# Normalising x on VectorE, squares of x by tokens, four-column gate scales and a new order in a hybrid attention and gMLP block

## The chip, the cores and the metric

The kernel runs on one core of one Trainium2 chip. The metric is the device time of one execution in microseconds (us). The engines are PE (TensorE), DVE (VectorE), ACT (ScalarE), POOL (GpSimd) and SP (SyncE, which here only issues DMA). PEld is the loading of weights into PE.

## The reference

One layer over 1024 tokens of width 1024, all in float32. The normalised stream is projected once and feeds attention (8 query heads and 2 key/value heads of 64), a gated MLP that mixes positions inside chunks of 128 tokens, and the merge gates:

```python
h = rmsnorm(x, norm_gain)
q, k, v, gate_a, u_in, v_in, gate_b, g_merge = split(h @ w_in)
q = axial_rope(rmsnorm(q, q_gain)); k = axial_rope(rmsnorm(k, k_gain))
attn = softmax(q k^T / 8) v * silu(gate_a)
y_a = attn @ w_proj_attn
vv = layernorm(gelu(v_in), ln_v_gain, ln_v_bias)          # 8 chunks x 8 groups
v_mix = einsum('gij,bcjgd->bcigd', w_spatial, vv) + b_spatial
gm = gelu(u_in) * v_mix * silu(gate_b)
y_b = gm @ w_proj_gmlp
g = sigmoid(g_merge + b_merge)
x = x + (g[0] * y_a + g[1] * y_b) @ w_out
return rmsnorm(x, final_gain)
```

## The kernel before

**Precision.** Each float32 operand of a large product is split into a rounded high part and a remainder (`split`, `split16`, L302 and L303: high on ACT, remainder on DVE), and each product is three matmuls (`mm3`, L188 to L190: high x high, high x low, low x high).

**Stages, in order of time.** Positions are those of the profiled execution.

1. 0 to 43 us: `load_x(dt)` brings x transposed (features on partitions, `xT`), eight tiles of 128 features. Each is multiplied by the norm gain and split (L164, L165). The k/v projection (`kv`) runs tile by tile in two of the three large PSUM tiles (tag `S`). `nat_weight` loads and splits the gMLP weights. `add_square` squares each transposed tile (L178 on ACT, L176 on POOL for tiles 1 and 4) and sums the squares on DVE (L182). One matmul per 128 tokens (L265) then adds over the features, and `power_rstd` gives `rstd`, the inverse root per token (DVE L139, POOL L140).
2. 43 to 86 us: `rB` is half of `rstd` spread over all partitions. `v_group(0..3)` project the gMLP input (PE, tile `v`), and their GELU on ACT (L481, scaled by `rstd`) frees the PSUM tile. `load_pair(k)` brings two tiles of `xT` again (`xp`), `norm_part(dt)` multiplies one by `rB` (DVE L315 for tiles 0, 1 and 3, two halves on POOL, L318, for the others), and `norm_split(dt)` turns it into two float16 parts (`x16`, L302 and L303). Beside them run the tables and the normalisation of k (`head_norm`, `rope`), and `v_post` (layernorm of a chunk) and `spatial` (its position mixing). `scales` loads weight blocks and sums their squares on ACT to scale them before the float16 split.
3. 86 to 160 us: `prep_q(dt)` splits the weights of q; `q_group(0..3)` need all eight `x16` tiles and all of those weights. `k_transposes`, `q_norm`, `q_split` prepare the attention operands. `bias_term` adds a row sum of the mixing matrix (L497) to the position bias (L501).
4. 160 to 405 us: 64 calls of `scores` (logits, softmax on DVE and ACT, DMA transpose) and 32 of `mix`, with the gate projections `run_fill` and the weight preparation `prep_next` between them.
5. 405 to 650 us: `proj_b`, `x_chunk`, then eight `gate(i)`. `pair_weights(i)` loads the gate weights and gets their scale from `unit_scale`: four sums of squares, one matmul each (L292), a copy (L294), and POOL steps (L295 to L298). `proj_a` and `merge` follow.
6. 650 to 747 us: `out_weight`, `split_y`, the output projection, residual and final norm.

**What sets the order.** The program text is a long hand-written list of calls at the end. The build's planner takes that order as a priority, simulates the engines' times, and fixes for every engine its own order of instructions; an engine then runs strictly in that order. `tc.high_priority()` moves a block ahead. Tiles with one tag share a small number of buffers, and a tile that needs a buffer waits until the last reader of an older one is done: `xa` (4 buffers: squares, raw weights of `scales`, x16 of tiles 0 to 3), `wraw` (4: raw weights), `qT` (4: `xp`, `vst`, later the transposed q), `ptr` (2: `nl`, then the split weights of q), `X` (8: the split x, then x16 of tiles 4 to 7), PSUM `S` (3), `o` and `z` (1 each). Nearly all loads are issued by SP in one queue; those of the first `scales` by ACT.

Of the kernel before, what the change touches and what calls it, by code (L numbers as in the profile page):

```python
# [16 lines left out]
P = 128  # L17
# [13 lines left out]
def hybrid_block_kernel(  # L31
# [79 lines left out]
    ones = t2("ones")[:, 0:P]  # L111
    dve.memset(ones, 1.0)

# [38 lines left out]
    def load_x(dt):  # L152
        raw = t4("T16", f"xraw{dt}")
        t = tX(f"xhl{dt}")
        hi, lo = t[:, 0, :], t[:, 1, :]
        cuts = [slice(0, 256), slice(256, 512), H(1)] if dt == 0 else [H(0), H(1)] if dt < 3 else [slice(0, 1024)]
        for i, r in enumerate(cuts):
            nc.sync.dma_start(out=raw[:, r], in_=xT[C(dt), r])
            if dt == 0 and i == 0:
                nc.scalar.dma_start(out=cs, in_=cst[:, 0:C_BSP])  # L160
            if dt == 0 and i != 1:
                first_w(i // 2)
        for r in cuts:
            act.activation(hi[:, r], raw[:, r], AF.Copy, scale=gain[:, dt:dt + 1])  # L164
            dve.scalar_tensor_tensor(out=lo[:, r], in0=raw[:, r], scalar=gain[:, dt:dt + 1], in1=hi[:, r].bitcast(F32),  # L165
                                     op0=ALU.mult, op1=ALU.subtract)
        xh.append(hi)
        xl.append(lo)
        xraw0.append(raw)

    ssq = []

    def add_square(dt):
        t = t4("xa", f"xsq{dt}")
        if dt in SQPOOL:
            pool.tensor_tensor(out=t, in0=xraw0[dt], in1=xraw0[dt], op=ALU.mult)  # L176
        else:
            act.activation(t, xraw0[dt], AF.Square)  # L178
        if dt == 0:
            ssq.append(t)  # L180
        else:
            (pool if dt in ADPOOL else dve).tensor_tensor(out=ssq[0], in0=ssq[0], in1=t, op=ALU.add)  # L182
# [23 lines left out]
    for i in range(4):  # L206
        for j in range(2):
# [16 lines left out]
            if dt > 0:  # L224
                add_square(dt - 1)
                nat_weight(W_VIN, dt - 1)
            if dt == 7:
                add_square(7)
                nat_weight(W_VIN, 7)
# [27 lines left out]
    dve.tensor_scalar(out=gsc[:, 0:1], in0=ssp[:, 16:17], scalar1=2.0 ** -16, scalar2=1e-30, op0=ALU.mult, op1=ALU.add)  # L257
# [4 lines left out]
    sst = ps_o("sst")  # L262
    for tt in range(NT):
        with tc.high_priority():
            pe.matmul(sst[:, tt:tt + 1], ssq[0][:, C(tt)], ones[:, 0:1], start=(tt == 0), stop=(tt == NT - 1))  # L265
    power_rstd(rstd, sst[:, 0:NT], NT, 1.0 / D)
# [20 lines left out]
    def unit_scale(ss, n, name, tag="sc", bufs=3):  # L287

        nscale.append(name)
        pt = ps_oz(len(nscale), f"us{name}")  # L290
        for i in range(n):
            pe.matmul(pt[:, 0:1], mscale.broadcast_to([P, P]), ss[:, i:i + 1], start=(i == 0), stop=(i == n - 1))  # L292
# [12 lines left out]
    x16, xpair = {}, {}  # L305
# [14 lines left out]
    NPD = (0, 1, 3)  # L320

    def norm_split(dt):
# [3 lines left out]
        else:  # L326
            if dt % 2 == 0:
                x16["t"] = tX16(f"x16{dt}")
            t = x16["t"][:, dt % 2]
# [165 lines left out]
    def bias_term(h):  # L495
        pt = ps_o(f"wsum{h}")
        pe.matmul(pt, ones, wsr[h], start=True, stop=True)  # L497
        for t in (2 * h, 2 * h + 1):
            for g2 in range(2):
                rows = slice(64 * g2, 64 * g2 + 64)  # L500
                dve.scalar_tensor_tensor(  # L501
                    out=bsp[rows, C(t)], in0=pt[rows, C(2 * (t % 2) + g2)], scalar=cs[rows, C_LNB + t:C_LNB + t + 1],
                    in1=bsp[rows, C(t)], op0=ALU.mult, op1=ALU.add)
# [460 lines left out]
    v_group(0)  # L964
# [18 lines left out]
    Ak, Bk = (heads(t) for t in tabk)  # L983
    load_wsp(0)
    early = scales(["q"] + order[:4], ["xa"] * 8)
    load_pair(1)
    load_wsp(1)
    load_pair(2)
    load_pair(0)
    norm_part(3)  # L990
    v_group(1)
    ktmp = t4("vS", "ktmp")
    head_norm(kn, ktmp, 0, 8, "kf")
    v_group(2)
# [5 lines left out]
    rope(kn, ktmp, Ak, Bk, 8, 2)  # L1000
    norm_part(0)
    norm_split(0)
    norm_part(1)
# [37 lines left out]
    dve.tensor_tensor(out=v3, in0=v3, in1=vinv[:, None, :].broadcast_to([P, 8, 128]), op=ALU.mult)
# [19 lines left out]
    norm_split(7)  # L1061
# [3 lines left out]
    split(khl[0], khl[1], kn, act)  # L1065
    q_group(0)
    v_post(3)
    spatial(2)
    qT = [t8("qT", 4, f"qT{j}") for j in range(4)]
    k_transposes(0)  # L1070
# [4 lines left out]
    k_transposes(2)
    spatial(3)
    scales(order[4:6])
    k_transposes(3)
    q_group(1)
    spatial(5)  # L1080
    prep_next()
    spatial(4)
    q_group(2)
    q_split(0)
    prep_next()
    q_split(1)
    v_post(6)
    spatial(6)
    scales(order[6:8])
    v_post(7)  # L1090
    q_norm(1)
    prep_next()
    q_split(2)
    spatial(7)
    q_group(3)
    prep_next()
    q_split(3)
    v_affine(1)
    v_affine(0)
    scores(*hs[0])  # L1100
    prep_next()
    v_affine(3)
    prep_next()
    scales(order[10:12])
    scores(*hs[1])
    scores(*hs[2])
    scales(order[8:10])
    scores(*hs[3])
    v_affine(2)
    run_fill(*halves[0])  # L1110
    prep_next()
    scores(*hs[4])
    q_norm(2)
    run_fill(*halves[1])
    q_split(5)
    scores(*hs[5])
    scores(*hs[6])
    mix(*hs[0][:2])
    q_split(4)
# [4 lines left out]
    q_norm(3)  # L1124
    scores(*hs[10])
    scores(*hs[11])
    q_split(6)
    q_split(7)
    mix(*hs[4][:2])
    scores(*hs[12])  # L1130
    scores(*hs[13])
    mix(*hs[6][:2])
    run_fill(*halves[2])
    mix(*hs[8][:2])
    scores(*hs[14])
# [142 lines left out]
    gate(6)  # L1278
    pws[7] = pair_weights(7)
# [3 lines left out]
    split_y(0)  # L1283
# [112 lines left out]
```

## Time and profile before

| | |
|---|---|
| median of 3 runs | 746.68 us (745.58 to 747.12) |
| profiled execution | 748.41 us, of which 746.6 us span |
| instructions | 12013 |
| busy: PE, DVE, ACT, POOL | 713.0, 591.8, 452.6, 132.3 us |
| mean granted TensorE clock | 0.983 |
| moved by DMA | 93.98 MB, 55.46 MB of it read from HBM |

Busy time is the time in which at least one instruction of the engine runs; waiting is not in it. The granted clock is the share of full speed that PE was given. The span is counted from the first to the last instruction. A row of the busy time by stage gives start, end, length, and then busy microseconds and the number of instructions for each engine. A row of the waits names who was idle, and for whose instruction.

### The profile page before, as it was taken

What the parts mean: (1) busy time and instruction counts of PE and PEld (TensorE: products, weight loads), DVE (VectorE), ACT (ScalarE), POOL (GpSimd) and SP (SyncE); (2) the same over time, 40 slices, a digit from 0 to 9 for tenths busy, and PEclk for the clock granted to TensorE, in tenths of its full rate; (3) what the DMA queues carried; (4) which work ended last, traced back from release to release, by engine and by line L of the source; (5) the groups of instructions that cost most, each with busy time, mean ns of one, the idle gap of its engine ahead of it and who ended that gap; (6) DMA issues with size and microseconds to landing.
All of it is one profiled execution on the core that took longest, in us unless ns stands there. A gap on an engine that the chain in (4) does not pass through costs nothing.

```text
span 746.6 us, 12013 instructions
## 1 busy us (share of the span) xinstructions
PE 713.0 (95%) x4685; PEld 471.2 (63%) x4685; DVE 591.8 (79%) x824; ACT 452.6 (61%) x808; POOL 132.3 (18%) x118
## 2 busy tenths in 40 slices
PE   7989879889999999999999999999999999999996
PEld 7978636455556555666656787556464466478885
DVE  7859989879989999777977699889687898972323
ACT  8563468887688898677785477655463445531011
POOL 3027731332301020001110025202002010000000
PEclk9999979999999999999999999999999999999999
DMA  8690144437487996998889921130031013330202
GB/s 309 224 356 7 57 140 155 129 113 141 88 176 144 205 196 114 160 164 141 156 150 219 270 85 45 41 127 16 1 141 57 1 56 128 135 137 26 110 32 84
DMA packets 156360, 93.98 MB, mean 126 GB/s; under 512 B 135824, under 2 KB 136464, under 8 KB 156304
## 3 DMA queue, kind: packets, MB, share of 16 engines
q1 hardware_dynamic: 154864, 88.75, 47.4%
q10 hardware_dynamic: 1440, 4.47, 1.7%
q8 instruction: 36, 0.59, 0.3%
q14 instruction: 20, 0.16, 0.1%
HBM read 55.46 MB, written 4.19 MB: 80 GB/s over the span
## 4 chain that ended last, share of the span: by engine, by line
PE 47%; DVE 20%; DMA 11%; ACT 10%; issue 7%; POOL 4%; SPq 1%; POOLq 0%; DVEq 0%; ACTq 0%
DMA T<-p 5%; PE out L189 4%; PE out L190 4%; PE out L188 4%; DVE p L651 4%; DVE nm L640 3%; PE g L188 3%; PE g L190 3%; PE g L189 3%; ACT p L650 2%; DMA sqq<-in_wall_dram 2%; DMA xraw<-in_xT_dram 2%; ACT P L644 2%; PE o L663 1%; DMA wraw<-in_wall_dram 1%
## 5 line engine op out<-in xcount | busy, mean ns | idle before, releaser
L651 DVE SCALAR_TENSOR_TENSOR p<-P,ri,p 128x1024 f16<-128x1024 f32 x64 | 83.4, 1307 | 18.2 <-ACT p L650 17.9
L644 ACT ACTIVATE P<-s,nm 128x1024 f32<-128x1024 f32 x64 | 71.2, 1113 | 27.6 <-DVE nm L640 23.6
L650 ACT ACTIVATE p<-P,ri 128x1024 f16<-128x1024 f32 x64 | 72.8, 1143 | 17.3 <-DVE ri L647 11.6
L640 DVE TENSOR_REDUCE nm<-s 128x1 f32<-128x1024 f32 x64 | 77.4, 1212 | 1.3 <-PE s L638 1.3
L637 PE MATMUL s<-kT,qT 128*128 128x512 f32 x128 | 56.7, 443 | 3.5 <-ACT P L644 2.7
L663 PEld LDWEIGHTS <-vS 128*64 128x64 f16 x1536 | 45.4, 110 | 18.0 <-issue 17.7
L663 PE MATMUL o<-T,vS 128*64 128x128 f16 x1536 | 52.8, 220 | 1.3 <-DMA T<-p 0.9
L638 PE MATMUL s<-kT,qT 128*128 128x512 f32 x128 | 50.8, 397 | 0.0
L923 ACT ACTIVATE sq<-xr 128x1024 f32<-128x1024 f32 x7 | 7.4, 1063 | 63.5 <-DVE xr L1326 63.2
L1326 DVE TENSOR_TENSOR xr<-out,xr 128x1024 f32<-128x1024 f32 x7 | 8.6, 1225 | 45.9 <-PE out L190 45.7
L295 POOL TENSOR_SCALAR scg<-scg 128x1 f32<-128x1 f32 x8 | 7.0, 871 | 190.7 <-ACT scg L294 110.4
L189 PE MATMUL out<-wo,yhl 128*128 128x512 f32 x96 | 37.4, 392 | 0.0
L188 PE MATMUL out<-wo,yhl 128*128 128x512 f32 x96 | 37.3, 392 | 0.0
L190 PE MATMUL out<-wo,yhl 128*128 128x512 f32 x96 | 37.3, 390 | 0.0
L188 PE MATMUL g<-x,wg 128*128 128x512 f16 x96 | 36.4, 379 | 0.0
L189 PE MATMUL g<-x,wg 128*128 128x512 f16 x96 | 36.4, 379 | 0.0
L190 PE MATMUL g<-x,wg 128*128 128x512 f16 x96 | 36.4, 379 | 0.0
L188 PE MATMUL q<-wq,x 128*128 128x512 f16 x64 | 25.5, 398 | 10.1 <-ACT vst L481 7.5
L637 PEld LDWEIGHTS s<-kT,qT 128*128 128x128 f32 x128 | 24.3, 190 | 12.1 <-ACT P L644 3.8
L188 PE MATMUL v<-nh,xhl 128*128 128x512 f32 x64 | 25.8, 403 | 2.5 <-DVE vn L238 2.5
L596 POOL TENSOR_TENSOR vm<-vm,ut 128x512 f32<-128x512 f32 x8 | 13.4, 1675 | 82.7 <-DVE ut L382 42.3
L302 ACT ACTIVATE wg<-graw,scg 128x512 f16<-128x512 f32 x16 | 11.6, 722 | 26.3 <-PE g L190 12.9
(548 smaller groups left out, 2113.4 us busy)
## 6 DMA issues: line engine op xcount, KB each, us to landing
wraw<-in_wall_dram SPq DMA_DIRECT2D x75, 256.0 KB, 3.3
graw<-in_wall_dram SPq DMA_DIRECT2D x16, 512.0 KB, 5.0
xraw<-in_xT_dram SPq DMA_DIRECT2D x13, 512.0 KB, 5.2
xp<-in_xT_dram SPq DMA_DIRECT2D x8, 512.0 KB, 8.7
wor<-in_wall_dram SPq DMA_DIRECT2D x8, 512.0 KB, 4.5
xr<-in_x_dram SPq DMA_DIRECT2D x8, 512.0 KB, 4.4
out_dram<-xr SPq DMA_DIRECT2D x7, 512.0 KB, 2.6
sqq<-in_wall_dram ACTq DMA_DIRECT2D x4, 512.0 KB, 5.8
```

What stands on the lines that cost most here:

```text
L188: pe.matmul(o, ah, bh, start=start, stop=False)
L189: pe.matmul(o, ah, bl, start=False, stop=False)
L190: pe.matmul(o, al, bh, start=False, stop=stop)
L302: act.activation(hi, raw, AF.Copy, scale=sc)
L596: pool.tensor_tensor(out=vm[:, et, H(h)], in0=vm[:, et, H(h)], in1=t, op=ALU.mult)
L637: pe.matmul(sp[:, H(hf)], qs, kT[v][:, 0, H(hf)], start=True, stop=False)
L638: pe.matmul(sp[:, H(hf)], qs, kT[v][:, 1, H(hf)], start=False, stop=True)
L640: dve.tensor_reduce(out=nm, in_=sp, axis=AX.X, op=ALU.max, negate=True)
L644: act.activation(Pt, sp, AF.Exp, bias=nm, accum_out=rsum)
L650: act.activation(hi, Pt, AF.Copy, scale=ri)
L651: dve.scalar_tensor_tensor(out=lo, in0=Pt, scalar=ri, in1=hi, op0=ALU.mult, op1=ALU.subtract)
L663: pe.matmul(ot[64 * h:64 * h + 64, 0:128], vS[:, kt, v, 64 * vl:64 * vl + 64], T[:, h, 8 * p + kt, :], start=(n == 0), stop=(n == len(part ...
```

## The change

The tokens' sums of squares are taken from x itself (tokens on partitions), loaded a second time in eight tiles; ACT squares and sums each, and neither DVE adds nor matmuls are left in it. All eight `norm_part` run on DVE. `unit_scale` does one matmul of four columns, and ACT sums the four columns while it copies. `bias_term` gets both 64-row halves of a tile in place with two masked matmuls of 256 columns, so that one DVE operation serves 128 rows. `gsc` has another constant (a scale). `x16` tiles 4 to 7 may be made in any order. The list of calls is reordered from `v_group(0)` to the output weights.

```diff
-    ones = t2("ones")[:, 0:P]
+    onz = t2("ones")[:, 0:P + 64]
+    ones = t2("one")[:, 0:P]
     dve.memset(ones, 1.0)
+    dve.memset(onz, 1.0)
+    dve.memset(onz[:, 64:P], 0.0)
...
-    def add_square(dt):
-        t = t4("xa", f"xsq{dt}")
-        if dt in SQPOOL:
-            pool.tensor_tensor(out=t, in0=xraw0[dt], in1=xraw0[dt], op=ALU.mult)
-        else:
-            act.activation(t, xraw0[dt], AF.Square)
...
-            (pool if dt in ADPOOL else dve).tensor_tensor(out=ssq[0], in0=ssq[0], in1=t, op=ALU.add)
+    ssx = const([P, NT], "ssx")
+    def add_square(tt):
+        xn = t4("xa", f"xn{tt}")
+        nc.sync.dma_start(out=xn, in_=x[C(tt), :])
+        act.activation(xn, xn, AF.Square, accum_out=ssx[:, tt:tt + 1])
...
             if dt > 0:
-                add_square(dt - 1)
                 nat_weight(W_VIN, dt - 1)
+            if dt > 3:
+                add_square(2 * dt - 8)
+                add_square(2 * dt - 7)
...
-    sst = ps_o("sst")
-    for tt in range(NT):
-        with tc.high_priority():
-            pe.matmul(sst[:, tt:tt + 1], ssq[0][:, C(tt)], ones[:, 0:1], start=(tt == 0), stop=(tt == NT - 1))
-    power_rstd(rstd, sst[:, 0:NT], NT, 1.0 / D)
+    power_rstd(rstd, ssx, NT, 1.0 / D)
...
-        for i in range(n):
-            pe.matmul(pt[:, 0:1], mscale.broadcast_to([P, P]), ss[:, i:i + 1], start=(i == 0), stop=(i == n - 1))
+        pe.matmul(pt[:, 0:n], mscale.broadcast_to([P, P]), ss, start=True, stop=True)
         sc = sb.tile([P, 2], F32, tag=tag, bufs=bufs, name=f"sc{name}")
-        act.copy(sc[:, 1:2], pt[:, 0:1])
+        act.activation(pt[:, 8:8 + n], pt[:, 0:n], AF.Copy, accum_out=sc[:, 1:2])
...
-    NPD = (0, 1, 3)
+    NPD = range(8)
...
-        pe.matmul(pt, ones, wsr[h], start=True, stop=True)
+        w4 = wsr[h].rearrange("p (t g i) -> p t g i", t=2, g=2)
+        for g2 in range(2):
+            pe.matmul(pt[:, 0:256], onz[:, 64 * g2:64 * g2 + P], w4[:, :, g2, :], start=(g2 == 0), stop=(g2 == 1))
         for t in (2 * h, 2 * h + 1):
-            for g2 in range(2):
-                rows = slice(64 * g2, 64 * g2 + 64)
-                dve.scalar_tensor_tensor(... 64 rows, 128 columns ...)
+            dve.scalar_tensor_tensor(... 128 rows, 128 columns ...)
```

The list of calls up to `q_group(0)`, before and after (calls that are not named stand where they stood):

```
before: v_group(0), tables, load_wsp(0), scales(q and 4 more), load_pair(1), load_wsp(1), load_pair(2), load_pair(0),
  norm_part(3), v_group(1), head_norm(k), v_group(2), scales_end, rope(k), norm_part(0), norm_split(0), norm_part(1),
  norm_split(1), v_group(3), norm_part(5), bias_term(0), v_post(0), spatial(0), v_post(1), spatial(1), bias_term(1),
  norm_split(3), prep_q(0..3), norm_part(2), prep_q(4), norm_part(4), prep_q(5), prep_q(6), norm_split(2), prep_q(7),
  norm_split(4), load_pair(3), norm_part(6), norm_split(5), norm_part(7), v_post(2), norm_split(6), norm_split(7), q_group(0)
after: tables, scales(q and 4 more), v_group(0), load_pair(1), load_pair(0), load_pair(2), v_group(1), load_wsp(0),
  load_wsp(1), norm_part(4), scales_end, norm_part(2), prep_q(0), norm_part(5), prep_q(1), head_norm(k), v_post(0),
  v_post(1), v_group(2), v_group(3), bias_term(0), prep_q(2), spatial(1), prep_q(3), rope(k), prep_q(4), norm_part(1),
  load_pair(3), norm_split(4), norm_part(6), norm_part(0), prep_q(5), norm_split(6), prep_q(6), norm_split(5),
  k_transposes(0), k_transposes(2), norm_part(7), prep_q(7), norm_part(3), norm_split(2), norm_split(3), k_transposes(3),
  norm_split(1), v_post(6), spatial(0), scales(2 more), v_post(3), norm_split(0), norm_split(7), q_group(0)
```

Behind it `v_post`, `spatial`, `q_norm`, `q_split`, `bias_term(1)` and `prep_next` are interleaved otherwise; `run_fill`, `mix`, `v_affine` and `scores` keep their own sequences and change places among each other; in the last stages `load_chunk`, `x_chunk`, `pair_weights`, `split_y` and `out_weight` move by a few places.

More of the change, by code (lines that the diff above doesn't have):

```diff
@@ L983, in hybrid_block_kernel @@
     Ak, Bk = (heads(t) for t in tabk)
+    early = scales(["q"] + order[:4], ["xa"] * 8)
+    v_group(0)
+    load_pair(1)
+    load_pair(0)
+    load_pair(2)
+    v_group(1)
     load_wsp(0)
-    early = scales(["q"] + order[:4], ["xa"] * 8)
-    load_pair(1)
     load_wsp(1)
[L988 to L994, printed above, removed]
+    norm_part(4)
     with tc.high_priority():
@@ L999, in hybrid_block_kernel @@
         dve.tensor_scalar(out=qc[:, 0:1], in0=qc[:, 1:2], scalar1=qc[:, 1:2], scalar2=1.0 / 64, op0=ALU.mult, op1=ALU.mult)
[L1000 to L1003, printed above, removed]
+    norm_part(2)
+    prep_q(0)
+    norm_part(5)
+    prep_q(1)
+    ktmp = t4("vS", "ktmp")
+    head_norm(kn, ktmp, 0, 8, "kf")
+    v_post(0)
+    v_post(1)
+    v_group(2)
+    v_group(3)
     v3 = vn.rearrange("p (t e) -> p t e", e=128)
@@ L1060, in hybrid_block_kernel @@
                              op0=ALU.mult, op1=ALU.subtract)
-    norm_split(7)
+    prep_q(5)
+    norm_split(6)
     kT = [tX(f"kT{v}") for v in range(2)]
@@ L1065, in hybrid_block_kernel @@
     split(khl[0], khl[1], kn, act)
+    prep_q(6)
+    norm_split(5)
+    k_transposes(0)
+    k_transposes(2)
+    norm_part(7)
+    prep_q(7)
+    qT = [t8("qT", 4, f"qT{j}") for j in range(4)]
+    norm_part(3)
+    norm_split(2)
+    norm_split(3)
+    k_transposes(3)
+    norm_split(1)
+    v_post(6)
+    spatial(0)
+    scales(order[4:6])
+    v_post(3)
+    norm_split(0)
+    norm_split(7)
     q_group(0)
[L1067 to L1070, printed above, removed]
+    v_post(2)
+    prep_next()
     v_post(4)
     k_transposes(1)
+    v_post(7)
+    spatial(2)
+    bias_term(1)
+    spatial(4)
     q_norm(0)
+    spatial(3)
+    q_split(0)
     v_post(5)
[L1075 to L1078, printed above, removed]
     q_group(1)
-    spatial(5)
[L1081 to L1092, printed above, removed]
+    q_group(2)
+    spatial(6)
+    q_norm(1)
+    spatial(7)
+    q_split(1)
+    scales(order[6:8])
+    spatial(5)
     q_split(2)
-    spatial(7)
-    q_group(3)
     prep_next()
     q_split(3)
-    v_affine(1)
-    v_affine(0)
+    prep_next()
+    prep_next()
+    prep_next()
+    q_group(3)
     scores(*hs[0])
-    prep_next()
-    v_affine(3)
+    v_affine(2)
+    scores(*hs[1])
+    scores(*hs[2])
+    run_fill(*halves[0])
+    scores(*hs[3])
+    scores(*hs[4])
+    scores(*hs[5])
+    q_norm(2)
+    q_split(5)
+    scores(*hs[6])
     prep_next()
     scales(order[10:12])
-    scores(*hs[1])
-    scores(*hs[2])
+    mix(*hs[0][:2])
+    v_affine(0)
+    q_split(4)
+    q_norm(3)
     scales(order[8:10])
[L1108 to L1119, printed above, removed]
     scores(*hs[7])
@@ L1128, in hybrid_block_kernel @@
     q_split(7)
-    mix(*hs[4][:2])
+    v_affine(1)
     scores(*hs[12])
     scores(*hs[13])
-    mix(*hs[6][:2])
-    run_fill(*halves[2])
-    mix(*hs[8][:2])
+    prep_next()
+    prep_next()
     scores(*hs[14])
@@ L1137, in hybrid_block_kernel @@
     scores(*hs[16])
+    mix(*hs[4][:2])
+    run_fill(*halves[1])
+    mix(*hs[6][:2])
+    mix(*hs[8][:2])
     mix(*hs[10][:2])
+    run_fill(*halves[2])
     scores(*hs[17])
     scores(*hs[18])
+    scores(*hs[19])
     mix(*hs[12][:2])
-    scores(*hs[19])
     mix(*hs[14][:2])
     run_fill(*halves[3])
+    mix(*hs[16][:2])
+    prep_next()
     run_fill(*halves[4])
-    prep_next()
-    prep_next()
     run_fill(*halves[5])
@@ L1191, in hybrid_block_kernel @@
     run_fill(*halves[14])
+    mix(*hs[36][:2])
+    run_fill(*halves[15])
+    scores(*hs[39])
+    scores(*hs[40])
     scores(*hs[41])
     scores(*hs[42])
-    mix(*hs[36][:2])
-    run_fill(*halves[15])
     scores(*hs[43])
@@ L1222, in hybrid_block_kernel @@
     scores(*hs[58])
-    mix(*hs[52][:2])
     run_fill(*halves[20])
     scores(*hs[59])
+    scores(*hs[60])
+    prep_next()
     run_fill(*halves[21])
-    scores(*hs[60])
     mix(*hs[54][:2])
     scores(*hs[61])
+    mix(*hs[56][:2])
+    mix(*hs[58][:2])
     scores(*hs[62])
-    mix(*hs[56][:2])
     scores(*hs[63])
-    mix(*hs[58][:2])
+    run_fill(*halves[22])
     gm_split(0)
     mix(*hs[60][:2])
-    run_fill(*halves[22])
     mix(*hs[62][:2])
@@ L1278, in hybrid_block_kernel @@
     gate(6)
+    split_y(0)
     pws[7] = pair_weights(7)
```

117 lines of the change are left out of this document (43 added, 74 removed).

## The prediction

> **What bounds the kernel now.** I read the page first, then busy time by stage, then the waits of PE, then the stretches of lowered clock, and last the chain of waits around the longest wait. From the page, busy time of each engine, and from the busy time by stage (start:end, length, then busy us and instructions of PE, PEld, DVE, ACT, POOL, granted clock, DMA share, GB/s):
>
> ```profile
> PE 713.0 (95%) x4685; PEld 471.2 (63%) x4685; DVE 591.8 (79%) x824; ACT 452.6 (61%) x808; POOL 132.3 (18%) x118
> ...
> 18.00:44.00 26.00, 26.00 (x180) 24.71 (x179) 18.44 (x23) 14.39 (x21) 2.51 (x2) 0.93 0.77 266
> 44.00:60.00 16.00, 13.49 (x65) 11.06 (x64) 12.88 (x19) 8.71 (x19) 2.98 (x3) 0.89 0.71 269
> 60.00:86.00 26.00, 26.00 (x117) 21.52 (x116) 23.07 (x30) 10.78 (x14) 21.79 (x20) 1.00 0.12 40
> 86.00:98.00 12.00, 4.46 (x30) 3.55 (x29) 11.93 (x15) 6.58 (x9) 8.71 (x6) 0.80 0.21 67
> 180.00:405.00 225.00, 218.34 (x2166) 133.71 (x2165) 197.25 (x250) 179.63 (x331) 28.41 (x17) 1.00 0.85 156
> 460.00:640.00 180.00, 179.64 (x851) 100.83 (x850) 154.61 (x234) 94.62 (x170) 19.09 (x28) 1.00 0.20 70
> ```
>
> PE is the bound. From 405 us on it is full, so a matmul taken out there shortens the end by its own length. In attention (180 to 405) it idles 225 - 218.34 = 6.66 us in small pieces. What an order can win lies before 180 us, in PE's waits (engine, line, waited for: us, times, longest) and in what follows them, the stretches at half clock:
>
> ```profile
> PE q L188 <- ACT vst L481: 7.5, 1, 7.5
> PE v L188 <- DVE vn L238: 2.5, 1, 2.5
> PE q L188 <- ACT qst L538: 2.5, 1, 2.5
> PE kv L189 <- DVE wl L124: 2.1, 1, 2.1
> ...
> 18.03:21.44 3.41, 3.41 (x17) 3.41 (x17) 3.41 (x3) 2.37 (x4) 0.83 (x1) 0.50 1.00 359
> 52.16:55.58 3.42, 3.42 (x10) 2.64 (x9) 3.18 (x3) 2.80 (x6) 1.75 (x2) 0.50 0.99 405
> 93.12:103.36 10.24, 5.81 (x14) 2.08 (x14) 10.09 (x18) 7.16 (x12) 3.70 (x3) 0.50 0.36 112
> 164.80:171.63 6.83, 6.83 (x24) 4.30 (x25) 6.74 (x14) 6.83 (x15) 5.40 (x8) 0.50 0.31 58
> ```
>
> The four waits are 14.6 us. PE was busy 3.41 + 3.42 + 5.81 + 6.83 = 19.47 us at clock 0.50, so some 9.7 us of work was lost besides. Each half-clock stretch begins within a few us of a wait.
>
> **The change part by part.**
>
> *Gate scales.* Eight pairs of gate weights each had four one-column matmuls, eight passes on PE; one matmul of four columns is two passes. In order of time on PE:
>
> ```profile
> 436.17 0.95 PE L292 MATMUL usg<-gss,mscale 128*128 128x1 f32 x8
> 436.98 0.48 PE L189 MATMUL yb<-gm,wh 128*128 128x512 f32 x1
> 37.09 1.84 PE L265 MATMUL sst<-ones,xsq 128*128 128x1 f32 x16
> 38.80 0.36 PE L188 MATMUL kv<-wh,xhl 128*128 128x256 f32 x1
> ```
>
> Eight passes hold PE for 436.98 - 436.17 = 0.81 us, 0.10 each; six fewer are 0.6 us, times eight pairs **-4.8 us**. They lie in the full stages, so I count all of it; the ends are 0 (if a pass were free beside its neighbours) and 8 x 0.81 = -6.5. ScalarE's copy becomes an activation with a sum, one accumulator read more, on an engine busy 94.62 of 180 us; hidden. If that cover failed, the scale would come later and the gate's weight split with it.
> The Trainium skill ("TensorE: Matmul & The Clock Gate", section "Wait — 56ns, not 53.3ns?") has small matmuls start no closer than about 25 ns; by that the 48 passes would be an estimated 1.2 us instead of 4.8 and the forecast 3.6 us later. The 0.10 per pass in the rows above disagrees with that floor.
>
> *Squares of x by tokens.* Out go 16 passes on PE (38.80 - 37.09 = 1.7 us), seven adds on VectorE, two squares on GpSimd. In come eight loads of 512 KB on SP's queue and eight ScalarE squares with sums instead of six without. VectorE in order of time, around the 2.1 us wait for wl:
>
> ```profile
> 11.89 1.21 DVE L182 TENSOR_TENSOR xsq<-xsq,xsq 128x1024 f32<-128x1024 f32 x1
> 14.68 1.21 DVE L182 TENSOR_TENSOR xsq<-xsq,xsq 128x1024 f32<-128x1024 f32 x1
> 15.82 0.68 DVE L124 TENSOR_TENSOR wl<-wraw,wh 128x512 fp32r<-128x512 f32 x1
> 17.02 2.92 DVE L165 SCALAR_TENSOR_TENSOR xhl<-xraw,cs,xhl 128x1024 fp32r<-128x1024 f32 x1
> 21.59 1.27 DVE L165 SCALAR_TENSOR_TENSOR xhl<-xraw,cs,xhl 128x1024 fp32r<-128x1024 f32 x1
> ...
> L182 DVE TENSOR_TENSOR xsq<-xsq,xsq x7: 1210/1212/1214, 11.9 to 32.3; 128x1024 f32<-128x1024 f32 x7
> ```
>
> Two adds of 1.21 stand ahead of wl in VectorE's order, so without them wl is ready 2.4 us earlier and the wait goes; with its half clock (3.41/2 = 1.7) and sst's 1.7 the v groups end some 5.5 us earlier than 86. I count this only once, below: what is late next is the first q matmul, which waits for VectorE and ScalarE, not for the v groups.
>
> *x normalised on VectorE.* Five of the eight multiplications by rB move from GpSimd (ten halves) to VectorE. Groups by form, then durations (min/median/max), then VectorE in order of time, each slow instance with a clean one:
>
> ```profile
> L318 POOL TENSOR_TENSOR xp<-xp,rB 128x512 f32<-128x512 f32 x10 | 14.7, 1501 | 7.7 <-DVE rB L283 7.7
> L303 DVE SCALAR_TENSOR_TENSOR x<-xp,gs,x 128x1024 f16<-128x1024 f32 x8 | 12.1, 1530 | 0.1
> L315 DVE TENSOR_TENSOR xp<-xp,rB 128x1024 f32<-128x1024 f32 x3 | 4.6, 1572 | 0.0
> ...
> L303 DVE SCALAR_TENSOR_TENSOR x<-xp,gs,x x8: 1261/1277/2382, 67.9 to 96.7; 128x1024 f16<-128x1024 f32 x8
> L315 DVE TENSOR_TENSOR xp<-xp,rB x3: 1199/1212/2306, 59.4 to 66.6; 128x1024 f32<-128x1024 f32 x3
> ...
> 62.80 1.67 DVE L124 TENSOR_TENSOR vl<-vst,vh 128x512 fp32r<-128x512 f32 x1 [0.69 <-ACT vh L118]
> 79.75 0.68 DVE L124 TENSOR_TENSOR vl<-vst,vh 128x512 fp32r<-128x512 f32 x1
> 52.78 2.21 DVE L1005 TENSOR_TENSOR vn<-vn,rstd 128x1024 f32<-128x1024 f32 x1
> 114.13 1.22 DVE L1041 TENSOR_TENSOR vn<-vn,vscr 128x1024 f32<-128x1024 f32 x1
> ```
>
> The moved work costs VectorE 5 x 1.21 = 6.05 us where it is 92% busy (60 to 98: 35.0 of 38). Against it, VectorE's operations are stretched while GpSimd multiplies: the eight L303 by 8 x (1530 - 1277) = 2.0 us, the three L315 by 3 x (1572 - 1212) = 1.1, vl by 1.0, vn by 1.0, in these rows 5.1, with more single cases near them. GpSimd's small rs and pow steps no longer queue behind 14.7 us of halves. Ends: +6.05 if no stretch goes, -2 if all that I see (about 8) goes. I take 0, nearest to the rows shown (6.05 - 5.1).
>
> *Bias term.* Eight VectorE operations on 64 rows become four on 128; one matmul of 512 columns becomes two of 256, as many columns on PE:
>
> ```profile
> L501 DVE SCALAR_TENSOR_TENSOR bsp<-wsum,cs,bsp x8: 322/350/359, 99.1 to 112.3; 64x128 f32<-64x128 f32 x8
> ```
>
> 4 x 0.35 = 1.4 us of VectorE, beside PE's q groups; counted 0 (its second half is moved behind q_group(0) altogether). The other matmuls keep their number. The masked columns need two more memsets at the start, on VectorE before data arrive: 0.
>
> *New order up to q_group(0).* The 7.5 us wait, as ScalarE's order of time and the chain of waits (start, us, what) have it:
>
> ```profile
> 95.63 0.72 ACT L302 ACTIVATE wq<-wraw,s0q 128x512 f16<-128x512 f32 x1 [4.75 <-DMA wraw<-in_wall_dram]
> 96.26 1.25 ACT L481 ACTIVATE vst<-v,rstd 128x512 f32<-128x512 f32 x2
> ...
> 92.06 0.65 DVE wq L303
> 92.73 2.88 DMA wraw<-in_wall_dram
> ```
>
> VectorE frees a wraw buffer late, SP reloads it, ScalarE sits 4.75 us on that load, and the GELU of v_group(3), which frees the PSUM tile that q_group(0) needs, stands behind it in ScalarE's order. The new order has prep_q(0) to prep_q(4) ahead of every norm_split, so the reload is asked for while VectorE and ScalarE have other work: **-4.75**. What is late next is x16 itself: norm_split(0) and (7) now come last, and eight L303 and eight L315 are over 19 us of VectorE, so I leave the other 2.8 us of this wait standing. Ends: -7.5, or 0 where x16 takes the load's place. Three k_transposes, four passes of 128 columns each, move ahead of q_group(0) into the idle: some 0.5 us each, **-1.5** (0 to -1.5). load_pair and wsp change places on SP's queue; both land long before 86 us, and VectorE and PE have other work till then.
>
> *New order behind it.* k_transposes, v_post, spatial, q_split and prep_next are interleaved otherwise, and so are scores, mix and fills. Of the 2.5 us wait for qst I take half, **-1.2** (0 to -2.5). In attention I count 0, bounds +-3.3, half of the 6.66 us idle. The half-clock stretches I leave as they are, since the waits before them only shrink. The later stages move out_weight, split_y and pair_weights by a step or two on full PE: 0.
>
> **Sum**: -4.8 - 4.75 - 1.5 - 1.2 = -12.25. The profiled execution took 748.41 us (span 746.6, 1.8 around it), and so 736.2 after. It stands 1.7 above the median of 746.68, which becomes 734.4.
>
> **The rivals.**
> *All front waits go.* For it: VectorE loses 8.5 us of adds, and each wait has its own cause. Against: they follow one another, the v groups ending earlier only makes PE wait for x16. Time: 14.6 of waits, 9.7 of half clock, 4.8 and 1.7 of matmuls, 746.7 - 30.8 = 716.
> The same Trainium skill page, section "HAM oscillation — how this bites in real kernels", has the clock drop only for idle gaps over about 3.4 us; here 2.1 and 2.5 us waits were followed by 3.4 us at 0.50, so the trace disagrees. By the page only the 7.5 us wait's half clock (5.81/2 = 2.9) would go with it, and this rival would give an estimated 723.
> *Only the matmuls count.* x16 takes the place of the weight load and other waits that of qst: 746.7 - 4.8 = 741.9, down to 740 with the transposes.
> *Slower: x arrives late a second time.* The eight x loads are 4.19 MB, at the 405 GB/s of the row above 10.3 us of transfer, in 18 to 60 us where the DMA share is already 0.77 and 0.71 (idle 6.0 + 4.6 = 10.6 us). They have to share four buffers, tag xa, with the eight sq loads. rstd needs all eight:
>
> ```profile
> 42.00 1.66 POOL L140 TENSOR_TENSOR rstd<-rstd,mhalf 128x8 f32<-128x8 f32 x1 [23.15 <-DVE rstd L139]
> ```
>
> If it comes 10 us after 43.7, then rB, the GELUs and x16 follow, and q_group(0) with them: +10.3 - 4.8 gives 752. It decides from a delay of 4.8 us. Against it: xT has landed by 24 us, so the loads may begin before 20, and the idle DMA time just holds them.
> *The change doesn't do what it says*, the planner keeping the old order of instructions: that falls under the second rival, since the matmuls go all the same.
>
> **How the numbers follow.** A measurement of this kernel tells about 0.2% (1.5 us) from no change. The forecast (728 to 739): 0.46. All front waits go, or most (712 to 728): 0.14. Only the matmuls (739 to 745): 0.17. A new wait eats just the matmuls' gain (745.2 to 748.2): 0.07. Slower, by late x or a worse place in attention (748.2 to 757): 0.16. So faster 0.77, same 0.07, slower 0.16. The range leaves about one in ten on either side: 717 to 750; the forecast's own is 728 to 739.
>
> **What would show it.** Right: usg has 16 passes, no sst; the stage 460 to 640 is some 4 us shorter with PE still full; no wait of kv for wl; L303 and L315 have medians and means alike; the first q matmul starts near 92 us, with less than 4 us of wait behind a DMA of wraw. Wrong: rstd later than 48 us; the first q matmul at 97 or later; PE idle in attention above 10 us; ScalarE's wait before wq no shorter.

## The result, and the profile after

The changed kernel takes **722.9 us** (median of 4 runs, 722.0 to 724.2) where the kernel before takes 746.18 (745.58 to 747.12): ratio 0.9688 [0.9666, 0.971], 23.3 us less. Forecast were 734.4, with 728 to 739 as the forecast's own range and 717 to 750 around it. The result lies in what the prediction called the rival "all front waits go", which it had worked out at 716.

The profiled execution took 724.2 us (span 722.4); that of the kernel before took 748.41, 2.2 above its median, so a part of what the two profiles differ by may be that one execution's own. From the page of the changed kernel, busy time of each engine:

```profile
PE 700.8 (97%) x4625; PEld 461.3 (64%) x4625; DVE 573.7 (79%) x820; ACT 455.7 (63%) x826; POOL 108.4 (15%) x106
```

Its busy time by stage, in the columns of the prediction's rows:

```profile
18.00:44.00 26.00, 24.23 (x160) 21.63 (x159) 13.54 (x24) 19.37 (x34) 1.65 (x1) 1.00 1.03 401
44.00:60.00 16.00, 16.00 (x80) 13.52 (x79) 15.87 (x25) 12.56 (x22) 5.43 (x5) 1.00 0.82 325
60.00:86.00 26.00, 26.00 (x134) 21.08 (x133) 25.45 (x37) 16.73 (x23) 7.13 (x9) 1.00 0.23 75
86.00:98.00 12.00, 10.90 (x61) 6.44 (x60) 11.23 (x25) 8.41 (x17) 5.75 (x9) 1.00 0.49 167
```

Where before had granted clocks of 0.93, 0.89 and 0.80 in the first, second and fourth of these stages, all four now stand at 1.00, and PE idles 1.1 us from 86 to 98 where it idled 7.5.

To see where the 24.2 us of span went, I cut both executions at the same two pieces of work: the first scores matmul and the first gate matmul (`g`). Busy time by these three stages, the kernel before first, the changed one second:

```profile
0.00:156.80 156.80, 140.24 (x770) 105.38 (x770) 128.01 (x188) 100.35 (x171) 54.00 (x48) 0.95 0.50 174
156.80:462.70 305.90, 295.76 (x2638) 190.44 (x2638) 265.11 (x353) 232.53 (x435) 54.88 (x34) 0.99 0.76 151
462.70:746.60 283.90, 277.00 (x1281) 175.35 (x1280) 198.73 (x284) 119.75 (x204) 23.47 (x36) 1.00 0.20 73
```

```profile
0.00:139.60 139.60, 133.67 (x757) 101.61 (x758) 113.53 (x184) 104.00 (x183) 29.95 (x36) 1.00 0.63 227
139.60:442.50 302.90, 293.81 (x2634) 189.22 (x2632) 265.23 (x356) 234.67 (x439) 59.62 (x38) 0.99 0.77 153
442.50:722.40 279.90, 273.36 (x1237) 170.51 (x1236) 194.97 (x281) 117.05 (x206) 18.79 (x32) 0.99 0.20 72
```

The front gave 156.8 - 139.6 = 17.2 us, the middle 3.0, the end 4.0. Of the front's 17.2, 10.6 are PE idle (16.6 to 5.9) and 6.6 are PE busy for less time (clock 0.95 to 1.00, and `sst` gone). VectorE's busy time to that point fell by 14.5 us, although five multiplications of 1.21 were moved onto it.

### The profile page after: what moved, and what is told of

Its sections match the earlier page's. It is cut to its first block, busy times and chain, and to the rows that moved or that the text cites. A ratio compares the mean times of both kernels' runs of the same rounds, so it can differ in the third digit from the quotient of the medians.

```text
span 722.4 us, 11893 instructions
## 1 busy us (share of the span) xinstructions
PE 700.8 (97%) x4625; PEld 461.3 (64%) x4625; DVE 573.7 (79%) x820; ACT 455.7 (63%) x826; POOL 108.4 (15%) x106
## 4 chain that ended last, share of the span: by engine, by line
PE 60%; DVE 14%; ACT 10%; DMA 8%; issue 4%; POOL 2%; SPq 1%; POOLq 0%; DVEq 0%; ACTq 0%
PE out L182 4%; PE out L183 4%; PE out L184 4%; DMA wraw<-in_wall_dram 4%; DVE nm L629 3%; DVE p L640 3%; PE g L182 3%; PE g L184 3%; PE g L183 3%; PE o L652 3%; DMA xraw<-in_xT_dram 3%; PE yb L184 2%; PE yb L182 2%; PE s L626 2%; PE yb L183 2%
## 5 line engine op out<-in xcount | busy, mean ns | idle before, releaser
L640 DVE SCALAR_TENSOR_TENSOR p<-P,ri,p 128x1024 f16<-128x1024 f32 x64 | 82.0, 1283 | 13.6 <-ACT p L639 13.2
L285 POOL TENSOR_SCALAR scg<-scg 128x1 f32<-128x1 f32 x8 | 4.4, 555 | 191.7 <-ACT usg L284 191.7
L626 PEld LDWEIGHTS s<-kT,qT 128*128 128x128 f32 x128 | 24.0, 188 | 11.4 <-ACT P L633 3.5
L627 PEld LDWEIGHTS s<-kT,qT 128*128 128x128 f32 x128 | 24.1, 188 | 4.3
L184 PE MATMUL yb<-gm,wl 128*128 128x512 f32 x64 | 26.1, 408 | 0.0
L182 PE MATMUL yb<-gm,wh 128*128 128x512 f32 x64 | 25.7, 401 | 0.0
L183 PE MATMUL yb<-gm,wh 128*128 128x512 f32 x64 | 25.4, 397 | 0.0
```

The lines of the kernel that those rows point to most:

```text
L182: pe.matmul(o, ah, bh, start=start, stop=False)
L183: pe.matmul(o, ah, bl, start=False, stop=False)
L184: pe.matmul(o, al, bh, start=False, stop=stop)
L626: pe.matmul(sp[:, H(hf)], qs, kT[v][:, 0, H(hf)], start=True, stop=False)
L627: pe.matmul(sp[:, H(hf)], qs, kT[v][:, 1, H(hf)], start=False, stop=True)
L640: dve.scalar_tensor_tensor(out=lo, in0=Pt, scalar=ri, in1=hi, op0=ALU.mult, op1=ALU.subtract)
```

## The experiments

Twelve kernels, all timed against the kernel before. "GELU" is the start of ScalarE's GELU of `v_group(3)`, which frees the PSUM tile of `q_group(0)` (96.26 in the prediction's row); "first q" is the start of the first q matmul; "front" the first scores matmul, "middle" from there to the first gate matmul, "end" from there to the end of the span.

| kernel | median us | ratio to before [95%] | GELU | first q | front | middle | end |
|---|---|---|---|---|---|---|---|
| before | 746.18 | 1 | 96.3 | 97.6 | 156.8 | 305.9 | 283.9 |
| changed | 722.9 | 0.9688 [0.9666, 0.971] | 79.4 | 82.9 | 139.6 | 302.9 | 279.9 |
| e1 new operations, old list | 734.29 | 0.9848 [0.9829, 0.9867] | 81.1 | 82.7 | 140.3 | 310.1 | 281.0 |
| e2 old operations, new list | 751.34 | 1.0065 [1.0039, 1.0091] | 93.4 | 94.7 | 157.4 | 306.9 | 285.1 |
| e3 changed, x on GpSimd again | 736.13 | 0.9871 [0.9853, 0.9889] | 83.6 | 84.9 | 148.8 | 306.0 | 280.1 |
| e4 changed, old squares | 745.83 | 1.0 [0.9983, 1.0017] | 87.8 | 89.9 | 155.3 | 305.4 | 281.8 |
| e5 changed, old gate scales | 729.39 | 0.9782 [0.976, 0.9804] | 79.7 | 83.1 | 140.3 | 302.1 | 285.9 |
| e6 before, x on VectorE | 741.99 | 0.9954 [0.9935, 0.9974] | 87.6 | 88.9 | 148.1 | 310.0 | 283.9 |
| e7 changed, gate weights later | 721.86 | 0.9679 [0.9656, 0.9703] | 79.9 | 83.4 | 140.6 | 300.1 | 280.7 |
| e8 before, new squares | 741.31 | 0.9942 [0.9923, 0.996] | 87.8 | 89.1 | 148.1 | 303.8 | 286.7 |
| e9 changed, idle adds on VectorE | 732.83 | 0.9826 [0.9808, 0.9844] | 81.6 | 83.9 | 143.3 | 305.9 | 281.8 |
| e10 changed, idle squares on GpSimd | 733.31 | 0.9834 [0.9813, 0.9855] | 82.1 | 83.5 | 145.4 | 305.7 | 281.8 |
| e11 changed, both | 738.73 | 0.9906 [0.9878, 0.9934] | 86.4 | 87.7 | 153.1 | 303.5 | 280.0 |
| e12 changed, old list from `load_chunk(0)` on | 723.0 | 0.9698 [0.9684, 0.9713] | 79.1 | 82.6 | 139.5 | 300.2 | 281.2 |

The columns from GELU on come from one execution of each kernel, and executions of one kernel lie up to 6 us apart (e2 747.8 to 754.0, e4 742.5 to 748.8), so 2 or 3 us in one stage of one kernel can be chance. Three results lie outside all that was expected of them: e2 and e4 are slower than either of their theories, and e3 costs 13.2 us where 5 to 10 were expected. In e7, e8 and e12 the rival came true. e1 and e9 follow one theory up to the first q matmul (B and C2) and neither in the total.

**The order or the operations: e1 and e2.** The functions of the one kernel with the list of calls of the other, both ways:

```diff
 # e1: functions as after
-(list of calls as after, from tables/v_group(0) to split_y(7))
+(list of calls as before, from v_group(0) to split_y(7))
 # e2: functions as before; x16 of tiles 4 to 7 may be made in any order
-(list of calls as before)
+(list of calls as after)
```

> All changed operations, the list of calls as it was before. Theory A (the order made the gain, the operations only their matmuls): 746.2 - 4.8 - 1.7 = about 740 us, first q matmul near 95 us, the clock at 0.50 after it. Theory B (relief of VectorE made the gain before 100 us, the order little): below 730 us, first q matmul near 85 us.

> The operations as before, the list of calls as after (x16 tiles 4 to 7 allocated in any order, as the new list needs). Theory A: 722.9 + 4.8 + 1.7 = about 729 us, first q matmul near 85 us. Theory B: about 740 us, since VectorE still does the adds and is stretched by GpSimd's halves, and the first q matmul stays near 95 us.

The front's gain comes with the operations alone (e1: 140.3), and not with the order alone (e2: 157.4). ScalarE in order of time shows why, e1 and then e2 (start, us, what, and in brackets the idle time before it and whom it waited for):

```profile
79.06 1.15 ACT L292 ACTIVATE x<-xp,gs 128x1024 f16<-128x1024 f32 x1 [4.19 <-DVE xp L305]
80.12 1.04 ACT L121 CAST khl<-kn 128x1024 fp32r<-128x1024 f32 x1
81.05 1.26 ACT L471 ACTIVATE vst<-v,rstd 128x512 f32<-128x512 f32 x2
```

```profile
85.51 1.15 ACT L302 ACTIVATE x<-xp,gs 128x1024 f16<-128x1024 f32 x1 [5.26 <-POOL xp L318]
86.57 1.03 ACT L118 CAST khl<-kn 128x1024 fp32r<-128x1024 f32 x1
89.42 1.15 ACT L302 ACTIVATE x<-xp,gs 128x1024 f16<-128x1024 f32 x1 [1.82 <-POOL xp L318]
91.08 0.72 ACT L302 ACTIVATE wq<-wraw,s0q 128x512 f16<-128x512 f32 x1 [0.51 <-DMA wraw<-in_wall_dram]
92.72 0.72 ACT L302 ACTIVATE wq<-wraw,s0q 128x512 f16<-128x512 f32 x1 [0.93 <-DMA wraw<-in_wall_dram]
93.35 1.25 ACT L481 ACTIVATE vst<-v,rstd 128x512 f32<-128x512 f32 x2
```

In e2 the new list does what the prediction said: ScalarE's wait for the weight reload shrinks from 4.75 us to 0.51 and 0.93. But ScalarE then waits 5.26 and 1.82 us for `xp` from GpSimd, and PE still waits 6.4 us for this GELU, by e2's waits:

```profile
PE q L188 <- ACT vst L481: 6.4, 1, 6.4
```

In e1, with the old list, no wait for the reload stands before the GELU at all: the GELU stands right behind the cast of `khl`, ahead of the load.

What the order does is in the middle. Busy time of e1 from the first scores to the first gate matmul, and PE's waits for the transposed probabilities, in the changed kernel, e1 and e2:

```profile
140.30:450.40 310.10, 295.49 (x2632) 189.47 (x2630) 266.85 (x354) 232.66 (x432) 52.22 (x34) 0.99 0.77 148
```

```profile
PE o L652 <- DMA T<-p: 0.7, 2, 0.4
```

```profile
PE o L652 <- DMA T<-p: 4.9, 5, 1.9
```

```profile
PE o L663 <- DMA T<-p: 6.1, 8, 1.9
```

PE idles 14.6 us in e1's middle against 9.1 in the changed kernel; 4.2 of these 5.5 us are waits for the transposes. By the medians the new list is worth 734.29 - 722.9 = 11.4 us with the new operations and costs 751.34 - 745.95 = 5.4 with the old ones (745.95 is the median of before in those runs). The planner lays out every kernel anew, so the list and the planner's answer to it aren't separated.

**The normalisation: e6 alone, e3 taken back.**

```diff
 # e6, in the kernel before
-    NPD = (0, 1, 3)
+    NPD = range(8)
 # e3, in the changed kernel
-    NPD = range(8)
+    NPD = (0, 1, 3)
```

> Before, with all eight norm_part on VectorE and nothing else changed. If the stretch that GpSimd's halves put on VectorE outweighs the 6 us added: the first q matmul 3 to 8 us earlier than 97.55, total 738 to 744. Rival (even, as the prediction had it, or the wait for the q weights stays): first q matmul within 2 us, total within 2 us of before.

> After, but with norm_part of tiles 2, 4, 5, 6 and 7 on GpSimd again. If GpSimd's halves stretch VectorE and that bounds the way to q: 5 to 10 us slower than after (728 to 733), means of the x split and the vl subtraction above their medians, q later by as much. Rival (the 6 us of VectorE saved and the stretch cancel out, as the prediction had it): within 2 us of after.

Alone it moves the front by 156.8 - 148.1 = 8.7 us, nearly all of it ahead of the first q matmul (97.6 to 88.9); taken back it costs 9.2 there and 13.2 in all. In e6 the group of the x split has no stretched instance left (busy, then mean ns: 1272 against 1530 before):

```profile
L303 DVE SCALAR_TENSOR_TENSOR x<-xp,gs,x 128x1024 f16<-128x1024 f32 x8 | 10.2, 1272 | 0.0
```

The same group in e3, from 44 to 98 us:

```profile
L293 DVE SCALAR_TENSOR_TENSOR x<-xp,gs,x 128x1024 f16<-128x1024 f32 x8 | 11.2, 1406 | 4.1 <-ACT x L292 4.1
```

ScalarE's wait for the halves in e3, and GpSimd in order of time there:

```profile
ACT x L292 <- POOL xp L308: 6.9, 2, 6.5
```

```profile
60.05 7.60 POOL L308 TENSOR_TENSOR xp<-xp,rB 128x512 f32<-128x512 f32 x4
...
78.82 0.20 POOL L360 TENSOR_TENSOR s1q<-s1q,s0q 128x5 f32<-128x5 f32 x1
78.98 3.54 POOL L308 TENSOR_TENSOR xp<-xp,rB 128x512 f32<-128x512 f32 x2
```

GpSimd's small scale step (L360) comes between halves, too. The stretch of the x split in e3 is small, 8 x (1406 - 1276) = 1.0 us. The larger thing up to the GELU is that a tile takes GpSimd two halves, over 3 us, where VectorE takes 1.22, and ScalarE waits 6.9 us for them. But only 2.0 of the 9.2 us lie ahead of the first q matmul (84.9 against 82.9). The other 7.2 lie between it and the first scores, where PE's longest wait is one for VectorE's copy of the transposed k:

```profile
PE ktp L508 <- DVE kT L515: 3.3, 1, 3.3
```

How the halves on GpSimd lead to that wait is not traced.

**The squares: e8 alone, e4 taken back.**

```diff
 # e8: the kernel before with the new add_square; e4: the changed kernel with the old one
-        t = t4("xa", f"xsq{dt}")
...                                      (squares of xT on ACT and POOL, 7 adds on DVE, 16 matmul passes)
+        xn = t4("xa", f"xn{tt}")        # x by tokens, loaded again
+        nc.sync.dma_start(out=xn, in_=x[C(tt), :])
+        act.activation(xn, xn, AF.Square, accum_out=ssx[:, tt:tt + 1])
```

> Before, with the squares of x by tokens alone. Theory C, formed on the second results (the squares are what the front gain hangs on): first scores matmul near 141 to 147 us instead of 156.8, total 733 to 738. Rival (it needs norm_part on VectorE too, or the gain is given back in attention, whose order was made for other times): first scores matmul near 150 or total above 740.

> After, but with the squares of x taken from the transposed tiles again (seven adds on VectorE, two squares on GpSimd, sixteen matmul passes, no second load of x). If the relief before 40 us reaches the end: +1.7 of matmuls, +2.1 wait for wl and +1.7 half clock, 5 to 6 us slower than after (728 to 729). Rival (absorbed by what q_group(0) waits for): at most 2 us slower.

Alone 8.7 us of the front, taken back 15.7, and 22.9 of the whole time: e4 is no faster than the kernel before. In e8, PE still waits 5.8 us for the GELU of `v_group(3)`, as the prediction said it would, but that GELU starts at 87.8 instead of 96.3, by the waits of PE and ScalarE's order of time:

```profile
PE q L179 <- ACT vst L469: 5.8, 1, 5.8
```

```profile
86.86 1.03 ACT L118 CAST khl<-kn 128x1024 fp32r<-128x1024 f32 x1
87.80 1.26 ACT L469 ACTIVATE vst<-v,rstd 128x512 f32<-128x512 f32 x2
```

The GELU moves by as much in e6 (87.6), and in both most of it is its place in ScalarE's order. The kernel before (up to the two rows that the prediction shows), then e6:

```profile
88.03 1.03 ACT L118 CAST khl<-kn 128x1024 fp32r<-128x1024 f32 x1
89.73 1.15 ACT L302 ACTIVATE x<-xp,gs 128x1024 f16<-128x1024 f32 x1 [0.67 <-POOL xp L318]
```

```profile
86.69 1.03 ACT L118 CAST khl<-kn 128x1024 fp32r<-128x1024 f32 x1
87.62 1.26 ACT L481 ACTIVATE vst<-v,rstd 128x512 f32<-128x512 f32 x2
```

Before, the GELU starts 8.2 us after the cast of `khl`, behind a split of x and the `wq` that waits for its reload. In e6, e8 and e1 it starts 0.9 us after that cast, and the load stands behind it. So 7.3 us of its move are the place; the cast itself comes 1.3 us earlier in e6, 1.2 in e8 and, with all the operations, 7.9 in e1 (80.12). The list is the same in all four: it is the planner that gave ScalarE another order once the operations were others. Why it did is not on record.

**What of the old squares costs: e9, e10, e11.** The changed kernel with work added that nothing reads: seven adds of 128x1024 on VectorE (e9), the two squares of tiles 1 and 4 on GpSimd (e10), both (e11; its scratch tiles hold buffers of `rB` and `vS`). x is squared by tokens, and loaded twice, in all three.

```diff
...
+            dve.tensor_tensor(out=scr[0], in0=scr[0], in1=xraw0[dt], op=ALU.add)        # e9, e11
...
+            pool.tensor_tensor(out=scr[1], in0=xraw0[dt], in1=xraw0[dt], op=ALU.mult)   # e11 (dt 1, 4); e10 into scr[0]
```

> After, with seven adds of 128x1024 on VectorE that nothing reads, in the places of the seven adds of squares (they read the raw x tiles and sum into the buffer of rB). Theory C1 (the adds' 8.5 us of VectorE made the old front slow): q_group(0) starts near 88 to 90 us as with the squares undone, total above 735. Rival C2 (it was GpSimd's two squares with the stretch, the sixteen matmul passes or the later rstd): within 3 us of after, q_group(0) near 83.

> After, with two squares on GpSimd of the raw tiles 1 and 4 that nothing reads (into the buffer of rB). The seven idle adds left the v groups' end at 80.3 us, with all squares undone it is 86.4. Theory D1 (GpSimd's two squares, by stretching VectorE and delaying wl, are most of that 6 us, with a wait of kv for wl and a half-clock stretch near 18 us): v groups end near 84 to 86. Rival D2 (alone they are absorbed): v groups end within 1.5 us of after's 79.3 and no half clock before 40 us.

> After, with the seven idle adds on VectorE and the two idle squares on GpSimd together, and x still by tokens. Theory D1 or D3 (both together make the wait for wl that before has): wait of kv for wl of 2 us, half clock near 18 us, v groups end near 85 us. Rival D4 (what the old way costs is in the matmuls for sst, the copies of v that wait behind it and the later rstd): v groups end within 2 us of the idle adds' 80.3.

The adds put 3.7 us on the front, the squares on GpSimd 5.8, both 13.5 of the 15.7 of e4, more than the two apart. So it is this work on the two engines, in the main; 2.2 us are left for the 16 matmul passes and for where x is read from. By the first q matmul, though, e9 and e10 cost only 1.0 and 0.6 us, e11 4.8 and e4 7.0: the rest of each lies between it and the first scores. In e10 these two waits of PE, the longest of its front, follow one another (`vscr` are the scales of v, `vh` a rounded part of it):

```profile
PE ktp L519 <- DVE vscr L1026: 2.2, 1, 2.2
PE sp L191 <- ACT vh L121: 1.8, 1, 1.8
```

They end at 101.5 us, and PE then runs at half clock until 107. In the changed kernel PE has other matmuls (`sp`) between the one that spreads `vscr` and this transpose of k (`ktp`), and does not wait for `vscr`. So a part of what e10 loses can be the planner's new order and not the squares themselves; this is not separated. What GpSimd's 4 us do directly shows in VectorE's groups up to 44 us, e9 and then e10, with GpSimd's own group of e10 last:

```profile
L168 DVE SCALAR_TENSOR_TENSOR xhl<-xraw,cs,xhl 128x512 fp32r<-128x512 f32 x5 | 3.7, 746 | 1.4 <-ACT xhl L167 1.4
```

```profile
L168 DVE SCALAR_TENSOR_TENSOR xhl<-xraw,cs,xhl 128x512 fp32r<-128x512 f32 x5 | 4.8, 958 | 2.8 <-ACT xhl L167 2.8
```

```profile
L186 POOL TENSOR_TENSOR scr<-xraw 128x1024 f32<-128x1024 f32 x2 | 4.1, 2038 | 12.1 <-DMA xraw<-in_xT_dram 12.1
```

The stretch is 5 x (958 - 746) = 1.1 us. The middle is 3 us longer in e9 and e10 as well.

**The gate scales: e5.**

```diff
-        pe.matmul(pt[:, 0:n], mscale.broadcast_to([P, P]), ss, start=True, stop=True)
+        for i in range(n):
+            pe.matmul(pt[:, 0:1], mscale.broadcast_to([P, P]), ss[:, i:i + 1], start=(i == 0), stop=(i == n - 1))
...
-        act.activation(pt[:, 8:8 + n], pt[:, 0:n], AF.Copy, accum_out=sc[:, 1:2])
+        act.copy(sc[:, 1:2], pt[:, 0:1])
```

> After, with four one-column matmuls and a copy per gate scale again. Theory (every pass taken out of a full PE counts): 48 passes of 0.10 us, 4.8 us slower than after, 727.7 us. Rival (a pass is free beside its neighbours, or the gate scale is late elsewhere): within 1.5 us of after.

It costs 6.5 us, next to nothing of it (0.7) in the front. The last stage of e5, in the columns above:

```profile
442.40:728.30 285.90, 277.65 (x1279) 175.12 (x1278) 195.45 (x281) 117.47 (x201) 25.52 (x36) 1.00 0.20 71
```

PE is busy 277.65 - 273.36 = 4.3 us longer with 42 more instructions (seven pairs of six): 0.10 a pass. The stage is 6.0 longer; 1.7 is idle time of PE besides.

**The one new wait, and the tail of the list: e7 and e12.** The changed kernel's waits of PE:

```profile
PE s L626 <- ACT P L633: 2.4, 3, 1.3
PE usg L282 <- ACT gsq L840: 2.0, 1, 2.0
PE qtp L451 <- DVE qs L443: 1.7, 1, 1.7
...
PE kv L183 <- DVE wl L127: 0.9, 1, 0.9
```

The place of the second in PE's order of time, and the stretch behind it, in the columns of the stages:

```profile
412.16 0.46 PE L282 MATMUL usg<-gss,mscale 128*128 128x4 f32 x2 [2.01 <-ACT gsq L840]
```

```profile
412.34:415.75 3.41, 3.41 (x10) 2.73 (x11) 3.41 (x5) 1.87 (x5) 1.37 (x2) 0.50 0.26 100
```

The first `pair_weights` is too early for PE: 2.0 us of wait, and 3.41/2 = 1.7 lost at half clock. e7 puts it two calls later; e12 has the list of before from `load_chunk(0)` on.

```diff
 # e7
-    pws[0] = pair_weights(0)      # behind x_chunk(1)
 ...
+    pws[0] = pair_weights(0)      # behind load_chunk(3)
 # e12
-(list as after, from load_chunk(0) to split_y(7))
+(list as before, from load_chunk(0) to split_y(7))
```

> After, with pair_weights(0) back behind load_chunk(3) in the list. In after PE waits 2.0 us at 410 us for ScalarE's sum of the first gate weights and then runs 3.4 us at half clock. Theory (this wait is a price of the new place): the wait and the half clock go, 2.0 + 1.7 = 3.7 us faster than after, about 719 us. Rival (what stands behind it, the gate scale on GpSimd, then comes late for gate(0)): within 1.5 us of after, or slower.

> After, with the list from load_chunk(0) to the output weights as it was before. With the whole old list the part behind the last mix took 311.2 us, in after 316.1. Theory: the new order of the last stages costs 4.9 us (the wait for the first gate weights with its half clock is 3.7 of it), and this kernel takes about 718 us. Rival: the last stages depend on what attention leaves, and it stays within 1.5 us of after.

In e7 the wait is 0.2 us and the middle 2.8 us shorter, but the medians differ by 1.0 us and the intervals overlap; e12 takes the same time as the changed kernel. So the tail of the list is worth nothing here, the order's 11.4 us lie ahead of `load_chunk(0)`, and no version is shown to beat the changed kernel.

## Why the prediction was right or wrong

The direction was right; half of the size was missing, and most of the parts stood in the wrong places. That e1, at 734.29, equals the forecast is chance: its terms were others.

- **Gate scales, -4.8: right.** 0.10 a pass held. Before to after, PE's busy time in the last stage fell by 3.6 us and the stage by 4.0 (seven of the eight pairs lie there: 4.2 expected); undone, +6.5. The Trainium skill's floor of about 25 ns between small matmuls ("TensorE: Matmul & The Clock Gate", section "Wait — 56ns, not 53.3ns?") would have given an estimated 1.2 for the 48 passes. As a lower bound that floor stands; as the price of a pass it is a quarter of what e5 and the trace of before show.
- **Squares, 0 beyond the v groups: wrong.** The v groups do end earlier, at 79.6 us in e8 against 86.3, where 5.5 us were worked out. The step that failed is "the v groups ending earlier only makes PE wait" for what is late next. What is late next was named rightly, but it was taken to stay where it was. It moved by 8.5 us (e8): 7.3 because the GELU no longer stood behind the `wq` reload in ScalarE's order, 1.2 because the cast ahead of it came earlier. So the load's 4.75 us, which the prediction read rightly in the trace but credited to the new list, went with the operations.
- **x on VectorE, 0 (-2 to +6): wrong, outside its ends.** Alone it gave 8.7 us of the front, by the same change of place (7.3 of 8.6 us of the GELU's move). The sum weighed VectorE's microseconds alone, 6.05 moved on against the stretches taken off, and held the order fixed. It also left out that x16 waits for the tile, and a tile takes over 3 us on GpSimd: that is ScalarE's 6.9 us of wait in e3 and 7.1 in e2. In the kernel before that wait was 0.7 us, so it is not what e6 took off.
- **New order up to q_group(0), -4.75 and -1.5: wrong, at its lower end of 0.** The reload came in time in e2 as worked out, and "x16 takes the load's place" came true there. With the new operations, the old list already reaches the first q matmul at 82.7 and the scores at 140.3.
- **New order behind it, -1.2, and attention, 0 +-3.3: too small.** With the new operations the middle is 7.2 us shorter by the new list, with the old ones 1.0 longer (e2), which is within the scatter. The bound was half of the idle time that the trace of before showed. e1's idle time, which the operations bring with the old list, is not in that trace.
- **Bias term and later stages, 0:** the later stages hold (e12). The bias term wasn't tried by itself.
- **The rival "all front waits go" is what happened,** 716 against 722.9: PE's idle time in the front fell by 10.6 us, and the front's half-clock stretches went (granted clock 1.00 in its row). Against it the prediction held that the waits follow one another, so that an earlier v group only waits longer. With the squares alone that is so (5.8 us of wait in e8); with all the operations no wait for that GELU is left (e1). The 723 that stands beside this rival meets 722.9 by chance: it kept 6.8 us of loss at half clock, and the changed kernel's front has none.
- **The slower rival fell.** The second load of x raises the DMA share from 18 to 44 us to 1.03, yet `rstd` is earlier, by GpSimd's row of the changed kernel (42.00 before):

```profile
38.52 1.65 POOL L143 TENSOR_TENSOR rstd<-rstd,mhalf 128x8 f32<-128x8 f32 x1 [29.06 <-DVE rstd L142]
```

- **What would show it:** `usg` has 16 passes, `sst` is gone, `wl` still costs kv 0.9 us in place of 2.1, and the two groups of the changed kernel (min/median/max) are as even as foretold. The first q matmul came at 82.9, not near 92:

```profile
L182 PE MATMUL q<-wq,x x64: 376/379/393, 82.9 to 139.1; 128*128 128x512 f16 x64
L293 DVE SCALAR_TENSOR_TENSOR x<-xp,gs,x x8: 1272/1276/1279, 57.6 to 80.0; 128x1024 f16<-128x1024 f32 x8
L305 DVE TENSOR_TENSOR xp<-xp,rB x8: 1214/1219/1220, 52.9 to 73.9; 128x1024 f32<-128x1024 f32 x8
```

The parts do not add up, and that is a result too. In the old list, squares (4.6), normalisation (3.7) and gate scales (4.0 in the last stage) make 12.3 us, near e1's 11.7. In the new list, undoing them costs 22.9, 13.2 and 6.5, together 42.6, far more than the whole change brought. A reading that fits is that the new list suits the times that the new operations give, and little else; it is not shown. Why its middle loses 2.5 to 3 us in e3, e4, e9 and e10, where only the front was touched, and 0.6 in e11, is open.

## What to carry to other kernels

Where a planner lays out every kernel anew, do not hold an engine's order fixed when pricing an edit: here the instruction that released the longest wait moved ahead of a load in three kernels with the old list (7.3 us each time), and two edits counted at nothing gave 8.7 us of the front each. Cost a move between engines also by how long the reader waits for the piece, not only by the busy time on either side. An order written for one set of operations can be a loss for another (here -11.4 and +5.4 us), so time both lists with both sets of operations before giving the order the credit.

## What the runs showed of the hardware

- The granted clock fell to 0.50 for 3.41 us after a PE wait of 2.0 us (412 us, changed kernel), while a wait of 1.7 us at 167 us in the same execution was not followed by it (clock 1.00 from 166 to 170). The Trainium skill ("TensorE: Matmul & The Clock Gate", section "HAM oscillation — how this bites in real kernels") puts the limit at about 3.4 us of idle; these runs disagree.
- With two GpSimd squares of about 2 us each beside them, VectorE's 128x512 splits took 958 ns on average (e10), without them 746 (e9).
- The DMA engines moved 401 GB/s on average over 26 us (18 to 44 us, changed kernel); `rstd`, which needs the eight loads of x among them, came at 38.5 us, where it came at 42.0 before without them.
